# Forget gate's sums brought to the scores by broadcast loads instead of TensorE passes, in a two-layer decoder trunk

## The chip, the cores and the metric

The kernel runs on one core of one Trainium2 chip, as one launch. The metric is the device time of that launch in microseconds (us). The profile shows one execution; the times are those of repeated runs without it. Engines are called as in the profile: PE (TensorE matmul, with PEld its weight loads), DVE (VectorE), ACT (ScalarE), POOL (GpSimd), SP (SyncE, which here only issues DMAs).

## The reference

A decoder trunk of two layers on 256 tokens of width 1024, in fp32. Layer 0 mixes by forgetting attention ("FoX"), layer 1 by MoBA with a relative-position bias. Each is followed by a SwiGLU feed-forward (width 2816) and a gated per-layer embedding; a last RMSNorm ends it. What this case touches is FoX: 16 heads of 64, and in each the logit of query t and key s carries the sum of the log forget gates between them.

```python
log_f = jax.nn.log_sigmoid(f_logit).transpose(0, 2, 1)
...
c = jnp.cumsum(log_f, axis=-1)
...
logits = jnp.einsum('bhqd,bhkd->bhqk', qblk, k).astype(jnp.float32) * scale
logits = logits + cq[..., None] - c[:, :, None, :]
logits = jnp.where(key_pos[None, :] <= t[:, None], logits, -jnp.inf)
probs = jax.nn.softmax(logits, axis=-1).astype(v.dtype)
```

The term `cq` is the same for a whole row and drops out of the softmax. What is left is one row of 256 sums per head, the same for all queries, and the causal mask.

## The kernel before

Every fp32 product is made of three matmuls of fp32r halves: each operand is split into a high and a low part, and high x high, high x low and low x high are added in PSUM (`mm3`, lines L95 to L97). The weights, 113 MB of them in raw form, stream from HBM all along: SP issues a load into `raw` (7 buffers), ACT copies it to `whi` (L170, L192, L140), DVE subtracts to get `wlo` (L176, L193, L143), six buffers each, and PE multiplies. So DVE's `wlo` subtractions stand among everything else that DVE does. One `wlo` per layer is made in two halves, the first by POOL (L172) and the second by DVE later (L173).

The engines take their instructions in the order in which the program leaves them; a scheduler sets that order, from the order of the code and from `tc.issue_after` (and `held`, a list of such marks), which put an instruction behind another one. A DMA stands in the queue of the engine that issues it: SP issues the weight loads, POOL the transfers of attention.

`attention(layer, ...)` treats the 16 heads as eight pairs. Per pair `j`:

- `project(j, 0)` and `project(j, 1)`: PE makes queries and keys of the pair (`pq`); DVE scales them to `qkt` (L578), ACT makes `qkh`, DVE `qkl` (L586).
- `scores(...)`: two pairs at once, behind the projections of pair 2, 4 and 6 (`BEHIND`), so that pairs 0 and 1, 2 and 3, 4 and 5 are done in the midst of the projections; pairs 6 and 7 come last. PE fills four banks `sp` (one per head); DVE's eviction (L624) adds a bias from SBUF, takes the row's minimum, and writes `e`; ACT makes the exponentials (L629) and their sums. The scores are negated throughout, so the minimum is the maximum.
- `scaled`: the reciprocal `rc` (L640) and the product with `e`, on ACT (L651), for pair 6 on DVE (L649).
- `turn`: DVE transposes 32 x 32 blocks (`turn`, L666, two instructions a pair). For pairs 0 to 4 POOL writes them to DRAM (`dt`, L677) and reads them back in four DMAs as `pt` (L681); for pairs 5 to 7 four DMAs go directly to `pt` (L673), by POOL, for pair 7 by SP.
- `values(j)`: PE multiplies `pt` with `v` for pairs j and j + 1 (`po`, L696 and L698), ACT and DVE split the result into `o` (L326, L327).
- `wo`: PE multiplies `o` with the output weights.

The last scores of pairs 6 and 7 are issued with `then=(0, 2)`: PE runs `values(0)` and `values(2)` right behind them, then a piece of `v`, then `wo` for the first pairs. DVE has the evictions of pairs 6 and 7, the splits of `po_0` and `po_2`, the scaling and turning of pairs 6 and 7 and the late half of `wlo` (L173) in that stretch.

In layer 0 the bias of L624 is only the mask `con[:, 0:256]`, whose first half is zero (first 128 columns) and whose second is the triangle. The sums come in by PE: `fox_bias`'s `summed` makes them along the 256 positions (`cum`, L410), ACT and DVE split them into `c` (L412, L414), POOL copies a part (L415), and `add` multiplies `c` by a selector `sel` that is one at the head's row, broadcast to all 128 outputs. This starts each bank `sp`:

```python
def add(i, sp):
    d = slice(i % 2 * DH, i % 2 * DH + DH)
    return mm(sp[:, 0:3 * P], sel[d, i:i + 1].to_broadcast([DH, P]), c[d], start=True, stop=False,
              skip_group_check=True)
```

A bank holds 384 columns: 128 for the first 128 queries with the first 128 keys, 256 for the later 128 queries. In layer 1 the bias is a loaded table (`bias1`), and no such pass is made.

Of the kernel before, what the change touches and what calls it, by code (L numbers as in the profile page):

```python
# [36 lines left out]
H = 16  # L37
# [34 lines left out]
CON = 9 * LINE  # L72
REL = 4 * P + H + 1
# [3 lines left out]
def trunk(ctx: ExitStack, tc: tile.TileContext, xg, wx, xr, pt, w, cst, gf, hot, out):  # L77
# [229 lines left out]
    mask, ident, wf32 = con[:, 0:2 * P], con[:, 2 * P:3 * P], con[:, 3 * P:4 * P].rearrange("p (k h) -> p k h", h=H)  # L307
    sel32, bfs = con[:, 4 * P:4 * P + H], con[:, 4 * P + H:4 * P + H + 1]
    nc.sync.dma_start(con, cst)
    first += [half() for _ in range(2)]  # L310
    sel = tiny.tile([P, H], F32R, bufs=1, name="sel")
    nc.gpsimd.tensor_copy(sel, sel32)
# [58 lines left out]
    def fox_bias(nm):  # L371
# [34 lines left out]
        def summed(f, a):  # L406
            with tc.issue_after(state["low"].ins):
                nc.vector.scalar_tensor_tensor(f, f, 0.0, a, op0=ALU.min, op1=ALU.subtract)
            cum = one.tile([P, S], F32, name="cum")
            nc.vector.tensor_tensor_scan(cum, f, zero, 0.0, ALU.add, ALU.add)  # L410
            c = one.tile([P, 3 * P], F32R, name="c")
            nc.scalar.activation(c[:, P:], cum, AF.Copy)  # L412
            for r in (slice(32, 64), slice(96, 128)):
                nc.vector.tensor_tensor(c[r, P:], cum[r], f32(c[r, P:]), op=ALU.subtract)  # L414
            nc.gpsimd.tensor_copy(c[:, 0:P], c[:, P:2 * P])  # L415

            def add(i, sp):
                d = slice(i % 2 * DH, i % 2 * DH + DH)
                return mm(sp[:, 0:3 * P], sel[d, i:i + 1].to_broadcast([DH, P]), c[d], start=True, stop=False,
                          skip_group_check=True)  # L420

            return (lambda i: (mask[:, P:], mask)), add
# [13 lines left out]
    def moba_bias():  # L436

        pb = bank("pb")
        mm(pb[:, :RVW], rr, hot2, start=True, stop=True)
        rv = work.tile([H, RVW], F32, tag="e", bufs=4, name="rv")  # L440
        nc.vector.scalar_tensor_tensor(rv, pb[:H, :RVW], -1.0, rm, op0=ALU.mult, op1=ALU.add)
        d1 = dram.tile([H, RVW], F32, name="d1")
        nc.sync.dma_start(d1, rv)
        d2 = [dram.tile([P, 4, RVW], F32, name=f"d2_{g}") for g in range(4)]
        bias = []

        def spread(g):
# [12 lines left out]

        return spread, load, (at, None)
# [12 lines left out]
    def attention(layer, nm, mid, early, nf):  # L474
        vb = [bank(f"v{layer}_{b}") for b in range(4)]
        rest, ahead = None, []
# [10 lines left out]
        for c in range(4):  # L487
            wt = [early.pop(0) if early else half() for _ in range(2 if c < 2 else 1)]
            for kk in range(2):
# [8 lines left out]
                if layer == 0 and k == KT - 2:  # L498
                    with tc.issue_after(got.ins), tc.issue_after(state["hi"].ins):
                        nm.spread(-0.125)  # L500
                        nm.column()
                        rest.gather()
                    tail = rest()
                    with tc.issue_after(state["hi"].ins):
                        ahead.append(blocks())
                    bias, add = tail()
# [89 lines left out]
        def scores(*js, then=()):  # L596
# [3 lines left out]
            if add:  # L600
                for i, _, _, sp in heads:
                    add(i, sp)
            for _, d, (t, _, _), sp in heads:
                mm(sp[:, 0:P], t[d, 0, 0:P], t[d, 1, 0:P], start=add is None, stop=True, skip_group_check=True)
# [5 lines left out]
            for i in then:  # L610
                with tc.issue_after(got.ins):
                    got = values(i)
                out = out or marks["o"]
            sl = (slice(0, P), slice(P, 3 * P))
            for n, j in enumerate(js):
# [4 lines left out]
                for s in range(2):  # L620
                    i, _, _, sp = heads[2 * n + s]
                    for q, b in enumerate(bias(i)):
                        with tc.issue_after(out[1].ins) if out and n and s else nullcontext():
                            marks["low"] = nc.vector.tensor_tensor_reduce(e[:, s, sl[q]], sp[:, sl[q]], b, 1.0, 3.0e38,  # L624
                                                                          ALU.add, ALU.min, mn[:, 0, s, q:q + 1])
# [11 lines left out]
        def inverse(j, mn):  # L637

            rc = tiny.tile([P, 2, 2], F32, tag="rc", bufs=4, name=f"rc{layer}_{j}")
            nc.vector.reciprocal(rc, mn[:, 1])  # L640
            return rc

        def scaled(j, e, mn):

            rc = inverse(j, mn)
# [8 lines left out]
        def turn(j, e):  # L654
# [8 lines left out]
            for s in range(2):  # L663
                src = e[:, s].rearrange("p (b y c) -> p b c y", b=3, c=4) if near else \
                      e[:, s].rearrange("p (b c x) -> p b c x", b=3, x=32)
                nc.vector.transpose(t[:, :, :, s].rearrange("p c b x -> p b c x"), src)  # L666
# [22 lines left out]
        def values(j):  # L689
# [9 lines left out]
            src = po.rearrange("p (j s) -> p j s", s=S)  # L699
            marks["o"] = ()  # L700
            for c in (slice(0, 1), slice(1, 2)) if j == 4 else (slice(0, 2),):
                at = slice(j + c.start, j + c.stop)
                marks["o"] += split(oh[:, at], ol[:, at], src[:, c])
            return got

        for j in range(NP):
            project(j, 0)
            if layer and j == 0:
# [5 lines left out]
                bias, add = mid(nm)()  # L714
# [3 lines left out]
            if j + 1 in BEHIND:  # L718
                got = scores(j - 2, j - 1)

# [40 lines left out]
        for x in fresh:  # L761
            scaled(*x)
            turn(*x[:2])
# [404 lines left out]
```

## Time and profile before

| | |
|---|---|
| timed runs, median (lowest to highest), 3 runs | 633.79 us (633.28 to 633.79) |
| the profiled execution's own time | 633.15 us |
| its span | 631.3 us |
| PE's granted clock, mean | 0.997 |
| moved by DMA | 135.34 MB, mean 214 GB/s |

Layer 0's attention lies in about the first 105 us of the span; the scores of layer 1 lie between 349 and 386 us. The columns of the rows below and in the prediction: in the page's groups and the timeline, line of the kernel, engine, operation, output <- input, shape, count, then (groups) busy us and mean ns of one, or (timeline, where start and duration stand first) in brackets the idle time before it and who ended it. An `x4` in the timeline stands for four instructions in a row. In the chain of waits a row has its start, its duration and the work that was the last to be waited for. In the rows of DMA issues the last number is the median time from issue to landing, in us.

```profile
PE   9999999999999999999999999999999999999995
DVE  6888987986666666668895899699666666666696
POOL 1103350000000000000000045100000000000011
DMA  9867968597766666665675598657766666665512
```

The span in forty slices (15.8 us each), busy tenths. POOL works in two places, the two attentions, and the DMA engines are at their fullest there too.

### The profile page before, as it was taken

The numbers are of one execution on the slowest core, as the hardware profiler recorded it, in microseconds if no ns is written. First come the engines' busy times: TensorE is split into PE (matmuls) and PEld (weight loads), VectorE is DVE, ScalarE is ACT, GpSimd is POOL, SyncE is SP. The second block draws the span as 40 slices with busy tenths as digits, with TensorE's granted clock in tenths as the row PEclk, the third lists the DMA queues.
The fourth block names the chain that finished last, engine by engine and source line by source line (L and its number), as shares of the span: only waits on it lengthen the run. The fifth ranks groups of instructions, "written<-read, shape, count | busy, mean of one in ns | idle before, by whom it ended". The sixth has DMA issues, their size and how long they took to land.

```text
span 631.3 us, 13134 instructions
## 1 busy us (share of the span) xinstructions
PE 623.3 (99%) x5259; PEld 603.9 (96%) x5259; DVE 469.1 (74%) x765; ACT 381.8 (60%) x658; POOL 47.5 (8%) x88
## 2 busy tenths in 40 slices
PE   9999999999999999999999999999999999999995
PEld 7899989999999999999989998999999999999985
DVE  6888987986666666668895899699666666666696
ACT  6768867854444445448774799578444444454653
POOL 1103350000000000000000045100000000000011
PEclk9999999999999999999999999999999999999998
DMA  9867968597766666665675598657766666665512
GB/s 337 297 204 228 282 191 288 177 343 272 241 196 198 193 192 211 198 212 177 193 224 183 199 298 252 213 205 266 240 194 185 199 198 202 196 210 181 168 44 91
DMA packets 41773, 135.34 MB, mean 214 GB/s; under 512 B 5152, under 2 KB 10672, under 8 KB 41712
## 3 DMA queue, kind: packets, MB, share of 16 engines
q1 hardware_dynamic: 37504, 124.18, 60.8%
q0 software_dynamic: 3488, 9.44, 5.1%
q10 hardware_dynamic: 720, 0.89, 0.5%
q8 instruction: 41, 0.67, 0.4%
q14 instruction: 20, 0.16, 0.1%
HBM read 126.07 MB, written 8.15 MB: 213 GB/s over the span
## 4 chain that ended last, share of the span: by engine, by line
PE 92%; DVE 4%; issue 1%; DMA 1%; POOL 1%; ACT 0%; SPq 0%; POOLq 0%; DVEq 0%; ACTq 0%
PE gu L96 13%; PE gu L95 13%; PE gu L97 13%; PE fo L97 6%; PE fo L96 6%; PE fo L95 6%; PE pq L95 5%; PE pq L97 5%; PE pq L96 5%; PE wo L95 2%; PE wo L97 2%; PE v L470 2%; PE wo L96 2%; PE v L95 2%; PE v L96 2%; PE v L97 2%
## 5 line engine op out<-in xcount | busy, mean ns | idle before, releaser
L176 DVE TENSOR_TENSOR wlo<-raw,whi 128x1024 fp32r<-128x1024 f32 (+1 forms) x168 | 203.4, 1216 | 61.1 <-ACT whi L170 61.0
L170 ACT ACTIVATE whi<-raw 128x1024 fp32r<-128x1024 f32 x168 | 175.7, 1056 | 87.9 <-issue 41.4
L96 PE MATMUL gu<-g,whi 128*128 128x256 f32 x704 | 194.6, 276 | 0.0
L95 PE MATMUL gu<-g,whi 128*128 128x256 f32 x704 | 194.6, 276 | 0.0
L97 PE MATMUL gu<-g,wlo 128*128 128x256 f32 x704 | 194.5, 276 | 0.0
L97 PEld LDWEIGHTS gu<-g,wlo 128*128 128x128 f32 x704 | 132.3, 188 | 0.0
L95 PEld LDWEIGHTS gu<-g,whi 128*128 128x128 f32 x704 | 132.2, 188 | 0.0
L96 PEld LDWEIGHTS gu<-g,whi 128*128 128x128 f32 x704 | 132.2, 188 | 0.0
L97 PE MATMUL fo<-fp,wlo 128*128 128x256 f32 x352 | 97.3, 276 | 0.0
L96 PE MATMUL fo<-fp,whi 128*128 128x256 f32 x352 | 97.2, 276 | 0.0
L95 PE MATMUL fo<-fp,whi 128*128 128x256 f32 x352 | 97.2, 276 | 0.0
L95 PE MATMUL pq<-g,whi 128*128 128x256 f32 x256 | 71.4, 279 | 0.0
L96 PE MATMUL pq<-g,whi 128*128 128x256 f32 x256 | 70.7, 276 | 0.0
L97 PE MATMUL pq<-g,wlo 128*128 128x256 f32 x256 | 70.7, 276 | 0.0
L193 DVE TENSOR_TENSOR wlo<-raw,whi 128x1080 fp32r<-128x1080 f32 x36 | 46.0, 1281 | 29.6 <-ACT whi L192 29.0
L95 PEld LDWEIGHTS fo<-fp,whi 128*128 128x128 f32 x352 | 66.1, 188 | 0.0
L96 PEld LDWEIGHTS fo<-fp,whi 128*128 128x128 f32 x352 | 66.1, 188 | 0.0
L97 PEld LDWEIGHTS fo<-fp,wlo 128*128 128x128 f32 x352 | 66.1, 188 | 0.0
L192 ACT ACTIVATE whi<-raw 128x1080 fp32r<-128x1080 f32 x36 | 39.4, 1102 | 26.8 <-PE gu L96 26.8
L95 PEld LDWEIGHTS pq<-g,whi 128*128 128x128 f32 x256 | 48.1, 188 | 0.9
L96 PEld LDWEIGHTS pq<-g,whi 128*128 128x128 f32 x256 | 48.1, 188 | 0.1
L97 PEld LDWEIGHTS pq<-g,wlo 128*128 128x128 f32 x256 | 48.1, 188 | 0.0
(199 smaller groups left out, 1048.9 us busy)
## 6 DMA issues: line engine op xcount, KB each, us to landing
raw<-w SPq DMA_DIRECT2D x177, 512.0 KB, 4.2
raw<-w SPq DMA_DIRECT2D x36, 540.0 KB, 4.0
dt<-turn POOLq DMA_DIRECT2D x10, 384.0 KB, 3.5
pt<-dt POOLq DMA_DIRECT2D x40, 96.0 KB, 5.4
d<-d SPq DMA_DIRECT2D x4, 768.0 KB, 6.7
bias<-d SPq DMA_DIRECT2D x4, 512.0 KB, 7.9
pt<-turn POOLq DMA_DIRECT2D x16, 96.0 KB, 3.0
pt<-turn SPq DMA_DIRECT2D x8, 96.0 KB, 2.9
```

The costliest lines, as they stand in the source:

```text
L95: mm(o, ah, bh, start=start, stop=False, skip_group_check=True)
L96: mm(o, ah, bl, start=False, stop=False, skip_group_check=True)
L97: return mm(o, al, bh, start=False, stop=stop, skip_group_check=True)
L170: state["hi"] = state[f"hi{i}"] = nc.scalar.activation(hi[:, c], raw[:, c], AF.Copy)
L176: state["low"] = nc.vector.tensor_tensor(lo[:, c], raw[:, c], f32(hi[:, c]), op=ALU.subtract)
L192: nc.scalar.activation(ht, raw[:, 0:WW], AF.Copy)
L193: state["lo"] = nc.vector.tensor_tensor(lt, raw[:, 0:WW], f32(ht), op=ALU.subtract)
L470: got = mm(bks[2 * t + hf], x[a][:, t * P:(t + 1) * P], w[b][:, hf * HC:(hf + 1) * HC], start=k + a + b == 0, stop=k + b == KT, skip_group ...
```

## The change

The passes `add`, the tensor `c` and the selector `sel` go, and with them the zero half of the mask (the constants shrink from 576 to 448 columns). In their place:

- POOL writes `cum[0:16]` (16 x 256) to a DRAM tensor `rows`.
- `load(j)`, once per pair: one SP DMA reads the two rows of the pair and broadcasts them to all 128 partitions (128 x 512, 256 KB) into a part of `h` (which is not yet used for anything else); the parts alternate with `j % 2`. Two POOL additions then put the mask on, one writing a copy for the first 128 queries (`first`), one in place (`both`).
- The eviction's bias is `first` and `both`; it adds sums and mask together.
- `load(0)` and `load(1)` follow the sums at once; `load(j)` and `load(j + 1)` follow the scores at j = 2, 4 and 6. The additions of these wait for the load, and the load for the evictions that read the same part before.

Beside that, for both layers, the work behind the last scores is put in another order: both evictions of `e_7` stand behind the split of `po_0`, whose ACT part now stands ahead of the exponentials; the split of `po_2` is put off until pair 6 has been turned, and pair 7 is turned behind it.

```diff
-            c = one.tile([P, 3 * P], F32R, name="c")
-            nc.scalar.activation(c[:, P:], cum, AF.Copy)
-            for r in (slice(32, 64), slice(96, 128)):
-                nc.vector.tensor_tensor(c[r, P:], cum[r], f32(c[r, P:]), op=ALU.subtract)
-            nc.gpsimd.tensor_copy(c[:, 0:P], c[:, P:2 * P])
...
-            return (lambda i: (mask[:, P:], mask)), add
+            rows = dram.tile([H, S], F32, name="rows")
+            nc.gpsimd.dma_start(rows, cum[0:H])
+            low = {}
+
+            def load(j):
+
+                part = h[:, j % 2 * 3:j % 2 * 3 + 3].rearrange("p m s -> p (m s)")
+                first = part[:, 0:S].rearrange("p (s k) -> p s k", k=P)
+                both = part[:, S:].rearrange("p (s k) -> p s k", k=S)
+                nc.sync.dma_start(both, bass.AP(tensor=rows.tensor, offset=rows.offset + 2 * j * S,
+                                                ap=[[0, P], [S, 2], [1, S]]))
+                for to, c in ((first, slice(0, P)), (both, slice(P, S))):
+                    nc.gpsimd.tensor_tensor(to[:, :, c], both[:, :, c], mask.unsqueeze(1).to_broadcast([P, 2, P]),
+                                            op=ALU.add)
+                for i in range(2):
+                    low[2 * j + i] = first[:, i], both[:, i]
+
+            return low.get, load
...
-                    bias, add = tail()
+                    bias, load = tail()
+                    for j in range(2):
+                        load(j)
...
-            if add:
-                for i, _, _, sp in heads:
-                    add(i, sp)
             for _, d, (t, _, _), sp in heads:
-                mm(sp[:, 0:P], t[d, 0, 0:P], t[d, 1, 0:P], start=add is None, stop=True, skip_group_check=True)
+                mm(sp[:, 0:P], t[d, 0, 0:P], t[d, 1, 0:P], start=True, stop=True, skip_group_check=True)
...
-                    got = values(i)
-                out = out or marks["o"]
+                    got = values(i, i != then[0])
+                out = marks["o"]
...
-                        with tc.issue_after(out[1].ins) if out and n and s else nullcontext():
+                        with tc.issue_after(out[1].ins) if out and n else nullcontext():
...
-                        with tc.issue_after(out[0].ins) if out and n == 0 and s else nullcontext():
+                        with tc.issue_after(out[0].ins) if out else nullcontext():
...
+            if late:
+                state["out"] = out
+            else:
+                out()
...
             if j + 1 in BEHIND:
                 got = scores(j - 2, j - 1)
+                for i in (j, j + 1) if load else ():
+                    load(i)
...
-        for x in fresh:
-            scaled(*x)
-            turn(*x[:2])
+        six, seven = fresh
+        scaled(*six)
+        rc = inverse(seven[0], seven[2])
+        with tc.issue_after(marks["rc"].ins):
+            turn(*six[:2])
+        with tc.issue_after(marks["turn"].ins):
+            state["out"]()
+        scaled(*seven, rc)
+        with tc.issue_after(marks["o"][1].ins):
+            turn(*seven[:2])
         state["late"]()
```

In the instruction lists below a number behind an underscore only tells tiles of one name apart; the pair is the first number of `dt_2`, `turn_2`, `e_4`, `po_2`. POOL's list in layer 0 between the transfers of pair 1 and those of pair 4, before:

```order
L681 DMA pt_1_668<-dt_1_669 32x4x192 x4
L677 DMA dt_2_873<-turn_2_869 128x768
L677 DMA dt_3_879<-turn_3_875 128x768
L681 DMA pt_2_872<-dt_2_873 32x4x192 x4
L681 DMA pt_3_878<-dt_3_879 32x4x192 x4
L677 DMA dt_4_1071<-turn_4_1067 128x768
```

and now:

```order
L684 DMA pt_1_671<-dt_1_672 32x4x192 x4
L421 TENSOR_TENSOR h<-h,con 128x256
L421 TENSOR_TENSOR h<-h,con 128x2x128
L421 TENSOR_TENSOR h<-h,con 128x256
L421 TENSOR_TENSOR h<-h,con 128x2x128
L680 DMA dt_2_878<-turn_2_874 128x768
L680 DMA dt_3_884<-turn_3_880 128x768
L684 DMA pt_2_877<-dt_2_878 32x4x192 x4
L684 DMA pt_3_883<-dt_3_884 32x4x192 x4
L421 TENSOR_TENSOR h<-h,con 128x256
L421 TENSOR_TENSOR h<-h,con 128x2x128
```

The four additions for pairs 4 and 5 stand ahead of `dt_2`, and those for pairs 6 and 7 ahead of `dt_4` (before pair 0's transfers stand eight more, for pairs 0 to 3).

DVE's list in layer 0 at the evictions of pairs 2 and 3 (`e_2` from the banks `sp_4` and `sp_5`), before:

```order
L586 TENSOR_TENSOR qkl_4_731<-qkt_4_728,qkh_4_730 128x384
L176 TENSOR_TENSOR wlo_841<-raw_839,whi_840 128x1024
L624 ISA e_2_758,mn_2_759<-sp_4_734,con 128x128
L624 ISA mn_2_759 128x1
L624 ISA e_2_758,mn_2_759<-sp_4_734,con 128x256
```

and now:

```order
L592 TENSOR_TENSOR qkl_4_734<-qkt_4_731,qkh_4_733 128x384
L627 ISA e_2_757,mn_2_758<-sp_4_737,h 128x128
L627 ISA mn_2_758 128x1
L627 ISA e_2_757,mn_2_758<-sp_4_737,h 128x256
L627 ISA mn_2_758 128x1
```

The evictions have moved ahead of one `wlo`, which now follows them; the same holds at the evictions of pairs 0 and 1 and of pairs 4 and 5.

DVE's list in layer 0 behind the last scores, from the first `wlo` behind the evictions of pair 7 to the late half L173, before:

```order
L176 TENSOR_TENSOR wlo_1184<-raw_1182,whi_1183 128x1024
L327 TENSOR_TENSOR o_336<-po_2_1151,o_336 128x2x256
L640 RECIPROCAL rc_6_1194<-mn_6_1163 128x4
L640 RECIPROCAL rc_7_1208<-mn_7_1173 128x4
L649 TENSOR_SCALAR e_6_1162<-e_6_1162,rc_6_1194 128x128
L649 TENSOR_SCALAR e_6_1162<-e_6_1162,rc_6_1194 128x256
L649 TENSOR_SCALAR e_6_1162<-e_6_1162,rc_6_1194 128x128
L649 TENSOR_SCALAR e_6_1162<-e_6_1162,rc_6_1194 128x256
L666 STREAM_TRANSPOSE turn_6_1200<-e_6_1162 128x3x4x32 x2
L666 STREAM_TRANSPOSE turn_7_1214<-e_7_1172 128x3x4x32 x2
L173 TENSOR_TENSOR wlo_1190<-raw_1188,whi_1189 128x512
```

and now:

```order
L176 TENSOR_TENSOR wlo_1185<-raw_1183,whi_1184 128x1024
L643 RECIPROCAL rc_6_1195<-mn_6_1164 128x4
L652 TENSOR_SCALAR e_6_1163<-e_6_1163,rc_6_1195 128x128
L652 TENSOR_SCALAR e_6_1163<-e_6_1163,rc_6_1195 128x256
L652 TENSOR_SCALAR e_6_1163<-e_6_1163,rc_6_1195 128x128
L652 TENSOR_SCALAR e_6_1163<-e_6_1163,rc_6_1195 128x256
L643 RECIPROCAL rc_7_1201<-mn_7_1174 128x4
L669 STREAM_TRANSPOSE turn_6_1203<-e_6_1163 128x3x4x32 x2
L325 TENSOR_TENSOR o_337<-po_2_1154,o_337 128x2x256
L669 STREAM_TRANSPOSE turn_7_1217<-e_7_1173 128x3x4x32
L173 TENSOR_TENSOR wlo_1191<-raw_1189,whi_1190 128x512
L669 STREAM_TRANSPOSE turn_7_1217<-e_7_1173 128x3x4x32
```

The split of `po_2` has gone behind pair 6's transposes, and L173 stands ahead of the last of the four transposes instead of behind it. On SP the four transfers of `pt_7` now stand behind one more weight load (540 KB).

More of the change, by code (lines that the diff above doesn't have):

```diff
@@ L71 @@
 GX = 64 + S
-CON = 9 * LINE
-REL = 4 * P + H + 1
+CON = 7 * LINE
+REL = 3 * P + H + 1
 @with_exitstack
@@ L306, in trunk @@
     con = one.tile([P, CON], F32, name="con")
-    mask, ident, wf32 = con[:, 0:2 * P], con[:, 2 * P:3 * P], con[:, 3 * P:4 * P].rearrange("p (k h) -> p k h", h=H)
-    sel32, bfs = con[:, 4 * P:4 * P + H], con[:, 4 * P + H:4 * P + H + 1]
+    mask, ident, wf32 = con[:, 0:P], con[:, P:2 * P], con[:, 2 * P:3 * P].rearrange("p (k h) -> p k h", h=H)
+    sel32, bfs = con[:, 3 * P:3 * P + H], con[:, 3 * P + H:3 * P + H + 1]
     nc.sync.dma_start(con, cst)
     first += [half() for _ in range(2)]
-    sel = tiny.tile([P, H], F32R, bufs=1, name="sel")
-    nc.gpsimd.tensor_copy(sel, sel32)
     rl = con[0:2 * BUCKETS, REL:REL + H]
@@ L410, in summed @@
             nc.vector.tensor_tensor_scan(cum, f, zero, 0.0, ALU.add, ALU.add)
-            c = one.tile([P, 3 * P], F32R, name="c")
-            nc.scalar.activation(c[:, P:], cum, AF.Copy)
-            for r in (slice(32, 64), slice(96, 128)):
[L414 to L420, printed above, removed]
-            return (lambda i: (mask[:, P:], mask)), add
+            rows = dram.tile([H, S], F32, name="rows")
[13 more added lines that the diff above has]
+            return low.get, load
         rest.gather = gather
@@ L459, in at @@
             return bias[0][:, i, P:2 * P], bias[0][:, i]
-        return spread, load, (at, None)
+        return spread, load, at
     def enter(bks, x, w, k):
@@ L475, in attention @@
         vb = [bank(f"v{layer}_{b}") for b in range(4)]
-        rest, ahead = None, []
+        rest, ahead, load = None, [], None
         def row(k, hf, w):
@@ L639, in inverse, with scaled @@
             rc = tiny.tile([P, 2, 2], F32, tag="rc", bufs=4, name=f"rc{layer}_{j}")
-            nc.vector.reciprocal(rc, mn[:, 1])
+            marks["rc"] = nc.vector.reciprocal(rc, mn[:, 1])
             return rc
-        def scaled(j, e, mn):
-            rc = inverse(j, mn)
+        def scaled(j, e, mn, rc=None):
+            rc = inverse(j, mn) if rc is None else rc
             for s in range(2):
@@ L665, in turn @@
                       e[:, s].rearrange("p (b c x) -> p b c x", b=3, x=32)
-                nc.vector.transpose(t[:, :, :, s].rearrange("p c b x -> p b c x"), src)
+                marks["turn"] = nc.vector.transpose(t[:, :, :, s].rearrange("p c b x -> p b c x"), src)
             p = work.tile([P, 4, 3, 2, 32], F32, tag="pt", bufs=4, name=f"pt{layer}_{j}")
@@ L687, in attention, with values @@
         pts = {}
-        def values(j):
+        def values(j, late=False):
             po = bank(f"po{layer}_{j}")
@@ L698, in values, with out @@
                     got = mm(o[d, P:S], v[:, 1, c], t[:, 2], start=False, stop=True, skip_group_check=True)
[L699 to L703, printed above, removed]
+            def out():
+                src = po.rearrange("p (j s) -> p j s", s=S)
+                marks["o"] = ()
+                for c in (slice(0, 1), slice(1, 2)) if j == 4 else (slice(0, 2),):
+                    at = slice(j + c.start, j + c.stop)
+                    marks["o"] += split(oh[:, at], ol[:, at], src[:, c])
+            if late:
+                state["out"] = out
+            else:
+                out()
             return got
@@ L713, in attention @@
                 keep(0)
-                bias, add = mid(nm)()
+                bias = mid(nm)()
             project(j, 1)
@@ L1142 @@
     hot, rvm = _buckets()
-    cst = np.concatenate([np.zeros((P, P), np.float32), tri, np.eye(P, dtype=np.float32),
+    cst = np.concatenate([tri, np.eye(P, dtype=np.float32),
                           fw[:, 3 * D:].reshape(KT, P, H).transpose(1, 0, 2).reshape(P, P),
```

## The prediction

> **What bounds the kernel now.** I read the page first (busy shares, chain), then the chain of waits in one score stage of each layer, then the timelines of PE, POOL and DVE through layer 0's attention, and last the DMA issues there.
>
> ```profile
> PE 623.3 (99%) x5259; PEld 603.9 (96%) x5259; DVE 469.1 (74%) x765; ACT 381.8 (60%) x658; POOL 47.5 (8%) x88
> PE 92%; DVE 4%; issue 1%; DMA 1%; POOL 1%; ACT 0%; SPq 0%; POOLq 0%; DVEq 0%; ACTq 0%
> ```
>
> PE is the bound: 99% busy and 92% of the chain. Taking a PE pass away therefore pays in full, as long as nothing PE needs then comes late. Everything below is that question.
>
> **The sum is made against the profiled execution**: 633.15 us, of which 631.3 is the span. The three timed runs have a median of 633.79 (633.28 to 633.79), so it lies 0.64 under the median. To speak of medians I add half of that, 0.3, to its result. A measurement of this kernel tells about 0.2% from no change, 1.27 us.
>
> **1. The sixteen passes go.** The chain through one score stage of layer 0, and through one of layer 1, which has no such passes, is what the new stage looks like:
>
> ```profile
> 53.33 0.54 PE sp L419 x4
> 53.88 0.45 PE sp L604 x8
> 54.32 0.71 PE sp L607 x12
> ...
> 362.36 0.65 PE sp L604 x8
> 363.01 0.71 PE sp L607 x12
> ```
>
> Layer 0's stage lasts 0.54 + 0.45 + 0.71 = 1.70 us, layer 1's 0.65 + 0.71 = 1.36: the first pass after the projections is slower, whichever it is. So a stage wins 0.34, less than the 0.54 that the passes take in the chain. Four stages: 4 x 0.34 = **-1.4 us**.
>
> The work that made `c` (ACT copy, two DVE subtractions, POOL cast) goes too. PE never waited for it, so I price it at nothing; the same for the smaller constant load and for the eviction's second operand, which is read from SBUF before and after.
>
> **2. Order behind the last scores.** Here is the one wait of PE in this attention, and what DVE does ahead of it:
>
> ```profile
> 88.97 0.28 PE L95 MATMUL wo<-o,whi 128*128 128x256 f32 x1
> ...
> 90.44 0.28 PE L96 MATMUL wo<-o,whi 128*128 128x256 f32 x1
> 91.15 0.38 PE L97 MATMUL wo<-o,wlo 128*128 128x256 f32 x1 [0.43 <-DVE wlo L173]
> 91.37 0.29 PE L95 MATMUL wo<-o,whi 128*128 128x256 f32 x1
> ...
> 87.35 3.17 DVE L666 STREAM_TRANSPOSE turn<-e 128x384 f32<-128x384 f32 x4
> 90.44 0.66 DVE L173 TENSOR_TENSOR wlo<-raw,whi 128x512 fp32r<-128x512 f32 x1
> ```
>
> Two steps take 0.93 us here and 0.23 elsewhere (matmuls start 0.11 apart), so 0.70 is lost. The new order puts one of the four transposes (3.17/4 = 0.79) behind L173. DVE's chain starts from the scores and so moves with PE; L173 then comes 0.79 earlier against PE and the wait goes: **-0.7 us**. Late next would be the split of `po_2` (`o`), which now stands behind the first two transposes, with the third between it and L173: L173 starts at 90.44 - 1.4 - 0.79 = 88.25, so the split ends at 87.46. PE begins the part of `wo` that reads it at 88.97 - 1.4 = 87.57, so this gain is all there is. In layer 1 no wait stands there and none is gained. In both layers `pt_7`'s four SP transfers now stand behind one more weight load (540 KB):
>
> ```profile
> 90.58 2.57 SPq L673 DMA_DIRECT2D pt<-turn  x4
> ...
> pt<-turn SPq DMA_DIRECT2D x8, 96.0 KB, 2.9
> ...
> 97.22 0.60 PE L696 MATMUL po<-pt,v 128*64 128x256 f32 x4
> ```
>
> The last one starts about 92.5 and lands at 95.4; PE reads at 97.2. Its transpose comes 1.4 earlier with the stage and 0.6 later for L173 ahead of it, so 94.6, plus up to 1.9 behind the load (540 KB at the 280 GB/s of the windows row in 5): 94.6 to 96.5, against 97.2 - 2.1 = 95.1 if PE waits nowhere. I price it at nothing in the forecast, since a wait in term 5 gives it room, with 1.4 as upper end.
>
> With nothing late the sum is -2.1 us, 631.05 on the profiled execution.
>
> **3. What is added.** Per pair: a broadcast load of 128x512 (256 KB) on SP and two POOL adds of 256 elements. No row shows such an add; the nearest are these, with a cast that ran alone and one that ran beside a two-input DVE instruction:
>
> ```profile
> 18.62 0.90 POOL L388 TENSOR_TENSOR qs<-quarters,qs 128x256 fp32r<-128x256 f32 x1 [4.65 <-ACT qs L387]
> 12.71 0.29 POOL L379 CAST add<-con 128x128 fp32r<-128x128 f32 x1
> 35.08 1.27 POOL L415 CAST c<-c 128x128 fp32r<-128x128 f32 x1 [14.65 <-DVE c L414]
> 34.98 1.23 DVE L176 TENSOR_TENSOR wlo<-raw,whi 128x1024 fp32r<-128x1024 f32 x1
> ```
>
> The same cast took 0.29 alone and 1.27 while DVE's subtraction ran, so a POOL instruction can sit out a whole DVE one. I take 0.90 for an add (same shape), with 0.6 and 1.3 as ends.
>
> The Trainium skill, "GPSIMD Engine Reference", section 3.1, speaks against this change: an elementwise add belongs on the Vector engine, and GpSimd needs about 2.6 cycles an element, by which 256 elements would be an estimated 0.55 us. That is less than the 0.90 of the trace; by the page the wait worked out in 5 would be 0.7 shorter.
>
> **4. The first pairs.** Their terms come from these rows:
>
> ```profile
> 31.79 0.69 DVE L410 TENSOR_TENSOR_SCAN cum<-f,zero 128x256 f32<-128x256 f32 x1
> 44.22 0.27 DVE L624 CUSTOM_DVE_ANT_0 e<-sp,con 128x128 f32<-128x128 f32 x1
> ...
> d<-rv SPq DMA_DIRECT2D x1, 24.0 KB, 2.3
> raw<-w SPq DMA_DIRECT2D x1, 512.0 KB, 3.6
> ```
>
> The sums are ready at 32.5. Writing 16 KB to DRAM, issue and landing (0.55 + 2.3) gives 35.4; a broadcast load at most as long as a 512 KB one, and the second queued right behind it, gives 39.4; four adds of 0.9 to 1.3 end between 43.0 and 44.6. The first eviction, which now stands ahead of one 1.2 us subtraction, would start at 43.1 and needs only the first pair's two adds (41.2 to 42). Cost: nothing, up to 1 us if the loads land in a crowd.
>
> **5. The later pairs, where POOL's queue decides.** The adds for pairs 4 and 5 now stand on POOL ahead of `dt_2<-turn_2`; behind that are `dt_3` and the eight `pt<-dt` that `values(2)` reads on PE.
>
> ```profile
> 55.81 1.23 DVE L176 TENSOR_TENSOR wlo<-raw,whi 128x1024 fp32r<-128x1024 f32 x1
> 58.83 0.42 DVE L624 CUSTOM_DVE_ANT_0 e<-sp,con 128x256 f32<-128x256 f32 x1
> ...
> 64.59 0.56 POOL L677 DMA_DIRECT2D dt<-turn  x1 [5.35 <-DVE turn L666]
> 65.52 0.56 POOL L677 DMA_DIRECT2D dt<-turn  x1 [0.36 <-DVE turn L666]
> 68.82 4.37 POOL L681 DMA_DIRECT2D pt<-dt  x8 [2.74 <-DMA dt<-turn]
> ...
> 79.89 0.60 PE L696 MATMUL po<-pt,v 128*64 128x256 f32 x4
> ...
> pt<-dt POOLq DMA_DIRECT2D x2, 96.0 KB, 6.5
> raw<-w SPq DMA_DIRECT2D x1, 512.0 KB, 5.9
> raw<-w SPq DMA_DIRECT2D x1, 512.0 KB, 7.7
> ...
> 68.00:74.00 6.00, 6.00 (x51) 5.91 (x51) 4.42 (x22) 5.39 (x20) 4.37 (x8) 1.00 0.93 280
> ```
>
> Before: the last of the eight starts at 68.82 + 7 x 0.55 = 72.6 and lands 6.5 later, at 79.1. PE reads pair 3 at 79.89: a margin of 0.8 us. PE now comes 1.4 earlier, at 78.5. If nothing else changed, the transposes would come two stages' worth (0.7) earlier and `pt_3` land at 78.4: margin nothing.
>
> After: pair 5's load reuses the buffer of pair 3, whose last eviction ended at 59.2. It now ends 0.7 earlier for PE and 1.2 earlier for the subtraction (55.81) that no longer stands ahead: 57.3. The load goes out then, among weight loads that took 5.9 and 7.7 us (issued at 55.4 and 57.1); I take 5.9, since it has half their bytes but queues behind them, with 3.6 and 7.7 as ends: landed at 63.2. Two adds, 1.8: 65.0. Then `dt_2` and, 0.6 later, `dt_3` at 65.6, where 65.52 was before. So `pt_3` lands at 79.2 rather than 78.4. The loads of pairs 6 and 7 (0.5 MB) go out near 69 to 70, into the stretch in which DMA is 93% busy at 280 GB/s: 1.9 us of all engines, half of it felt by the transfers that share them, 0.9. Landed: 80.1. PE waits 80.1 - 78.5 = **+1.6 us**. The ends: no wait; and 65.0 + 2.6 for slow adds = 67.6, `dt_3` 68.2, `pt_3` at 81.8, with all 1.9 us felt 83.7, a wait of 5.2.
>
> While PE waits there, L173 and `po_2` have that much more room, so term 2 stays. Pairs 6 and 7 get their adds after `pt_3`'s issues; a late `e_7` has the same room. Later `dt_4` and `pt_4`, two to three us late, are read only 15 us after. The weight loads behind SP's new waits are used some 10 us or more after their issue: nothing.
>
> **Sum**: -1.4 - 0.7 + 1.6 = -0.5 us, 632.65 profiled, **633.0 us** as a median.
>
> **The rivals.**
>
> *The waits stay hidden (faster).* If pair 5's load lands in 4 us and the adds take 0.6, POOL is free before the transposes are done, the wait at `values(2)` is under 0.8, and `pt_7` is not late by more. Time: between -2.1 and -1.3, 631.4 to 632.2. For it: the load has half a weight load's bytes, and the eight `pt` of the first pairs leave the DMA sooner or later than assumed. Against it: a margin of nothing even without a delay.
>
> *DVE and POOL hold each other up (slower).* These rows are one operation on DVE, in layer 0 beside POOL's subtraction and in layer 1 without it:
>
> ```profile
> 85.36 2.07 DVE L649 TENSOR_SCALAR e<-e,rc 128x128 f32<-128x128 f32 x4
> 85.99 1.29 POOL L172 TENSOR_TENSOR wlo<-raw,whi 128x512 fp32r<-128x512 f32 x1 [2.15 <-DVE e L649]
> ...
> 392.98 1.01 DVE L649 TENSOR_SCALAR e<-e,rc 128x128 f32<-128x128 f32 x4
> 393.90 3.19 DVE L666 STREAM_TRANSPOSE turn<-e 128x384 f32<-128x384 f32 x4
> ...
> 393.85 1.30 POOL L172 TENSOR_TENSOR wlo<-raw,whi 128x512 fp32r<-128x512 f32 x1 [1.07 <-DVE e L649]
> ...
> 44.00:80.00 36.00, 36.00 (x337) 34.14 (x337) 31.36 (x91) 31.07 (x87) 12.42 (x23) 1.00 0.84 258
> ```
>
> DVE lost 1.06 us to 1.29 us of POOL. If each add costs DVE as much of its own length, 0.74, the twelve adds between 44 and 80 us cost it 8.9; by the windows view DVE is busy there for 31.36 of 36 us, idle for 4.6, so it would fall 4.3 behind and PE with it: -2.1 + 4.3 = +2.2, **635.6**. It decides once more than (4.6 + 2.1 + 1.3)/12 = 0.67 us of each add falls on DVE. For it: most of DVE's time there is two-input subtractions. Against it: evictions and transposes are in between (layer 1's POOL subtraction at 393.85 left the four transposes at 3.19, against 3.17 in layer 0), and most adds wait for DVE instead of holding it. The Trainium skill, "SBUF — State Buffer", section "Who interferes with whom", gives the rule: a DVE instruction with two SBUF inputs and a GpSimd instruction that reads SBUF share a read port, and whichever issues first keeps it. The trace agrees (1.27 for 0.29, 2.07 for 1.01).
>
> *POOL's queue at its slow end (slower)* is case 5's upper end, +1.3 to +3.1: 634.8 to 636.6.
>
> *The change doesn't do what it says*: no; the passes are gone from PE's program, and only the price of what replaces them is open.
>
> **How the numbers follow.** A small wait at `values(2)` that eats most of the gain (between -1.3 and +1.3): 0.42; hidden: 0.36; DVE and POOL together 0.12; queue's slow end 0.10. So faster 0.36, same 0.42, slower 0.22. The likeliest case alone spans 632.2 to 634.7. The range takes in the hidden case to its floor, 633.15 - 2.1 + 0.3 = 631.35, and the slower cases up to DVE's price: 631.3 to 635.6; what lies beyond is 1 in 10.
>
> **What would show it.** Score stages of layer 0 of 1.36 us (term 1); no wait on L173 (term 2); first eviction not waiting for POOL (4); `pt_3` landing near 80 and PE waiting at `po` L696 near 78.5 (5); adds near 0.9 us, DVE's subtractions still near 1.2. I am wrong if PE does not wait at L696 although `dt_2` is late, or waits for `wlo` in the projections instead.

## The result, and the profile after

The changed kernel is slower: a median of 639.88 us in six runs (638.02 to 641.90) against 633.51 for the kernel before in its six, a ratio of 1.0109 with a 95% interval of 1.0097 to 1.0120. That is 6.4 us between the medians and 6.9 by the ratio, outside the range of 631.3 to 635.6. It was run once more beside later experiments:

> The changed kernel once more on the chip of these runs, for a comparison on one chip and a second trace: 638 to 642 us, the wait before pair 2 or 3 in layer 0 between 5 and 8 us, and any further loss at another place, layer 1 among them.

1.0079 (1.0051 to 1.0108), with waits of 4.6 and 1.2 us before pairs 2 and 3 in layer 0 and none in layer 1. All ratios are of fast runs; of the seven runs of "`dt` first" below, one took 1620.93 us and is not in its ratio. The profiled execution took 640.03 us, its span 638.2 (before: 633.15 and 631.3).

The page of the changed kernel: busy shares, the granted clock of PE in forty slices, the shares of the chain, and the DMA issues of the new loads.

```profile
PE 623.7 (98%) x5243; PEld 602.7 (94%) x5243; DVE 469.0 (73%) x763; ACT 382.1 (60%) x657; POOL 61.9 (10%) x103
...
PEclk9999979999999999999999999999999999999999
...
PE 84%; DVE 6%; DMA 5%; issue 2%; POOL 1%; ACT 1%; SPq 1%; POOLq 0%; DVEq 0%; ACTq 0%
...
h<-rows SPq DMA_DIRECT2D x8, 256.0 KB, 6.0
```

Sixteen matmuls are gone, but PE's busy time has not fallen and DMA has taken 5% of the chain. The place is one: from the first projection to `values(4)` PE needed 71.4 us before (23.8 to 95.2) and 78.4 now (23.3 to 101.7); what follows lasts as long as before (536.1 and 536.5 us to the end of the span).

PE's timeline at the values behind the last scores:

```profile
75.15 0.71 PE L607 MATMUL sp<-qkt 64*128 64x128 f32 x8
...
76.51 0.65 PE L699 MATMUL po<-pt,v 128*64 128x256 f32 x4
...
83.44 1.12 PE L699 MATMUL po<-pt,v 128*64 128x256 f32 x4 [5.41 <-DMA pt<-dt]
...
85.47 1.12 PE L699 MATMUL po<-pt,v 128*64 128x256 f32 x4 [0.48 <-DMA pt<-dt]
```

The score stage lasts 76.51 - 75.15 = 1.36 us, as forecast. Then PE stands before pair 2 until 83.44 and before pair 3 until 85.47, waiting for the transfers that POOL issues. POOL's timeline shows why they are late:

```profile
63.68 4.91 POOL L421 TENSOR_TENSOR h<-h,con 128x256 f32<-128x256 f32 x4 [4.61 <-DMA h<-rows]
68.54 1.13 POOL L680 DMA_DIRECT2D dt<-turn  x2
75.13 4.37 POOL L684 DMA_DIRECT2D pt<-dt  x8 [5.46 <-DMA dt<-turn]
```

POOL waits 4.61 us for a load, spends 4.91 on the four additions of pairs 4 and 5, and only then issues `dt_2` and `dt_3`, 3.95 us later than before (64.59). These take longer too, and the eight `pt` go out at 75.13 instead of 68.82.

The wait costs more than its length. The windows view (PE busy, then further engines, with PE's granted clock third from the end) and the matmuls show it:

```profile
75.00:80.00 5.00, 3.03 (x37) 2.21 (x36) 4.10 (x7) 3.62 (x7) 4.85 (x9) 1.00 1.00 321
80.00:85.00 5.00, 1.55 (x8) 0.85 (x8) 4.31 (x20) 4.07 (x17) 4.67 (x9) 0.71 0.92 273
85.00:90.00 5.00, 4.53 (x17) 3.33 (x18) 3.81 (x9) 2.63 (x6) 2.93 (x6) 0.61 0.82 235
90.00:95.00 5.00, 5.00 (x42) 4.83 (x42) 4.64 (x6) 3.27 (x4) 3.04 (x5) 1.00 0.66 162
```

With PE idle the clock that it is granted falls to 0.71 and then 0.61 for the first work behind the wait; the four passes at 85.47 take 1.12 us where the same took 0.60 before.

### The profile page after: what moved, and what is told of

The parts are those of the page before. It is cut to its first block, busy times and chain, and to the rows that moved or that the text cites. A ratio compares the mean times of both kernels' runs of the same rounds, so it can differ in the third digit from the quotient of the medians.

```text
span 638.2 us, 13150 instructions
## 1 busy us (share of the span) xinstructions
PE 623.7 (98%) x5243; PEld 602.7 (94%) x5243; DVE 469.0 (73%) x763; ACT 382.1 (60%) x657; POOL 61.9 (10%) x103
## 2 busy tenths in 40 slices
DMA packets 42957, 137.39 MB, mean 215 GB/s; under 512 B 5296, under 2 KB 10960, under 8 KB 42896
## 4 chain that ended last, share of the span: by engine, by line
PE 84%; DVE 6%; DMA 5%; issue 2%; POOL 1%; ACT 1%; SPq 1%; POOLq 0%; DVEq 0%; ACTq 0%
PE gu L96 13%; PE gu L95 13%; PE gu L97 13%; PE fo L97 6%; PE fo L96 6%; PE fo L95 6%; PE pq L95 3%; PE pq L96 3%; PE pq L97 3%; PE wo L95 2%; PE wo L97 2%; PE wo L96 2%; DVE wlo L176 2%; PE v L95 2%; PE v L96 1%
## 5 line engine op out<-in xcount | busy, mean ns | idle before, releaser
L95 PE MATMUL pq<-g,whi 128*128 128x256 f32 x256 | 71.4, 279 | 0.0
```

What stands on the lines that cost most here:

```text
L95: mm(o, ah, bh, start=start, stop=False, skip_group_check=True)
```

## The experiments

Three theories, with what each names as the cause; the expectations call them theory 1, 2 and 3. **Queue** (1): POOL's additions for pairs 4 and 5 wait for their loads and hold `dt_2` and `dt_3` behind them. **Bytes** (2): 2 MB of broadcast loads crowd the other transfers. **Hold-up** (3): POOL's additions and DVE's two-input instructions make each other wait. From here on every run is told as its ratio to the kernel before, measured beside it (there its medians were 632.8 to 633.0 us; 0.0010 is 0.63 us). Each run left one profiled execution, and its place among the run's times is said where it lies at an end.

| run | POOL's additions | bytes of the loads | ratio (95% interval) |
|---|---|---|---|
| change, first set | ahead of `dt_2` | all | 1.0109 (1.0097 to 1.0120) |
| change, second set | ahead of `dt_2` | all | 1.0079 (1.0051 to 1.0108) |
| `dt` first | behind `dt_3` | all | 1.0051 (1.0030 to 1.0072) |
| no additions | none | all | 1.0021 (1.0007 to 1.0036) |
| no loads | ahead of `dt_2` | pairs 0, 1 | 1.0014 (1.0003 to 1.0026) |
| short loads, `dt` first | behind `dt_3` | pairs 0, 1 | 0.9994 (0.9984 to 1.0003) |
| short loads, no additions | none | pairs 0, 1 | 0.9969 (0.9960 to 0.9979) |
| no passes, nothing instead | none | none | 0.9968 (0.9956 to 0.9980) |
| new order alone | (before) | none | 0.9986 (0.9977 to 0.9995) |
| six buffers, early | behind `dt_1` and `dt_3` | all | 1.0004 (0.9995 to 1.0013) |
| six buffers, late additions | behind `dt_3` and `pt_3` | all | 0.9999 (0.9989 to 1.0010) |

### The two gains

The kernel before without its passes:

```diff
-            if add:
-                for i, _, _, sp in heads:
-                    add(i, sp)
...
-                mm(sp[:, 0:P], t[d, 0, 0:P], t[d, 1, 0:P], start=add is None, stop=True, skip_group_check=True)
+                mm(sp[:, 0:P], t[d, 0, 0:P], t[d, 1, 0:P], start=True, stop=True, skip_group_check=True)
```

> The kernel before without its sixteen PE passes and with nothing in their place (the forget gate's sums are left out of the scores). What the passes cost alone. By my first term: each score stage of layer 0 lasts 1.36 us instead of 1.70, together -1.4 us. The wait for the late half of wlo stays about as it is, so the time is 632.0 to 632.4 us against 633.5. If PE then finds pair 3's transposed scores not there (they would land at 78.4 against 78.5), some of it is lost.

0.9968, which is -2.0 us (-2.8 to -1.3). The chain through the same score stage as in the prediction:

```profile
52.34 0.65 PE sp L601 x8
52.99 0.71 PE sp L604 x12
```

1.36 us for 1.70. From the first projection to `values(4)` it is 2.1 us shorter than before. That is more than the -1.4 expected, because the wait for the late half of `wlo` is gone as well: PE waits nowhere up to 110 us.

The kernel before with only the new order behind the last scores:

```diff
-                    got = values(i)
-                out = out or marks["o"]
+                    got = values(i, i != then[0])
+                out = marks["o"]
...
-        for x in fresh:
-            scaled(*x)
-            turn(*x[:2])
+        six, seven = fresh
...
+        with tc.issue_after(marks["turn"].ins):
+            state["out"]()
+        scaled(*seven, rc)
+        with tc.issue_after(marks["o"][1].ins):
+            turn(*seven[:2])
```

> The kernel before with only the new order behind the last scores, passes kept. By my second term: PE's wait of 0.43 us (0.70 lost) for the late half of wlo in layer 0 goes, -0.7 us, 632.8 us. A rival: the split of po_2, put off behind two transposes, comes late for PE instead, and the time is that of before.

0.9986, -0.9 us (-1.5 to -0.3). PE's steps at the place of the wait are 0.11 us all along:

```profile
89.85 0.28 PE L96 MATMUL wo<-o,whi 128*128 128x256 f32 x1
89.96 0.28 PE L97 MATMUL wo<-o,wlo 128*128 128x256 f32 x1
90.07 0.28 PE L95 MATMUL wo<-o,whi 128*128 128x256 f32 x1
```

The rival (a late `po_2`) fell. But the two gains do not add up to more than the first alone brought: without passes the wait went by itself, and the run with both (short loads, no additions) has 0.9969.

### Bytes and additions, one at a time

The changed kernel without its additions (the causal mask of layer 0 is left out):

```diff
-                for to, c in ((first, slice(0, P)), (both, slice(P, S))):
-                    nc.gpsimd.tensor_tensor(to[:, :, c], both[:, :, c], mask.unsqueeze(1).to_broadcast([P, 2, P]),
-                                            op=ALU.add)
...
-                    low[2 * j + i] = first[:, i], both[:, i]
+                    low[2 * j + i] = both[:, i, 0:P], both[:, i]
```

> The changed kernel without its sixteen POOL additions: the loads stay, the evictions read the loaded rows directly, and the causal mask of layer 0 is left out. Theory 1 (POOL's queue: the additions for pairs 4 and 5 wait for their loads and hold up dt_2 and dt_3 behind them): dt_2 is issued near 63.7 us instead of 68.5, pt_3 has landed by 79 to 80.5, PE waits 0.5 to 2 us before the values of pair 3 instead of 7, and the time is 631.5 to 633.5 us. Theory 2 (traffic: 2 MB of loads crowd the transfers, whoever issues them): dt_2 goes out on time, but its transfers still land late, pt_3 after 82, and the time is 635.5 us or more. Theory 3 (DVE and POOL hold each other up at SBUF): as theory 1 in time, since POOL computes nothing there, and DVE's wlo of 1.50 us beside the additions goes back to 1.28.

1.0021: between the two. `dt_2` went out on time, at 63.79, and PE still waited, 0.4 us before pair 2 and 0.8 before pair 3. DMA issues from 63 to 70 us (KB each, median us to landing), first of this run, then of the run without passes:

```profile
dt<-turn POOLq DMA_DIRECT2D x2, 384.0 KB, 5.9
```

```profile
dt<-turn POOLq DMA_DIRECT2D x2, 384.0 KB, 2.8
```

The same two transfers, issued half a microsecond apart in the two runs (63.79 and 63.28), take twice as long when the loads are there. So bytes cost something by themselves, or the weight loads do that wait behind the loads on SP. The next run separates these: the same waits, but 8 partitions instead of 128 for pairs 2 to 7.

```diff
-                nc.sync.dma_start(both, bass.AP(tensor=rows.tensor, offset=rows.offset + 2 * j * S,
-                                                ap=[[0, P], [S, 2], [1, S]]))
+                n = P if j < 2 else 8
+                nc.sync.dma_start(both[0:n], bass.AP(tensor=rows.tensor, offset=rows.offset + 2 * j * S,
+                                                     ap=[[0, n], [S, 2], [1, S]]))
```

> The run without additions, with the loads of pairs 2 to 7 cut from 128 to 8 partitions (16 KB instead of 256 KB each), so that SP's queue has the same waits in the same places and the weight loads behind them go out as late, but 1.4 MB less is moved. The causal mask is left out, and the sums of most rows are those of an earlier pair. Traffic (bytes): 630.5 to 631.5 us, dt lands in about 3 us. The hold-up of the weight loads behind SP's new waits: still 633 to 635, with dt at 5 to 6 us.

0.9969, with `dt` landing in 3.3 us and no wait of PE in either attention. It is the bytes, not SP's queue: 1.0021 - 0.9969 = 0.0052, 3.3 us. ("Bytes" takes in the number of packets, which falls with them, from 42957 to 42189; these runs don't tell the two apart.) The traces, both near the middle of their runs, show 2.4 us between them (633.72 and 631.27). Of these, 1.6 lie between the first projection and `values(4)` of layer 0 (71.0 and 69.4 us) and 0.9 are a wait of PE in layer 1, which comes up again below.

The other half: all additions in their place, the loads of pairs 2 to 7 left out.

```diff
-                nc.sync.dma_start(both, bass.AP(tensor=rows.tensor, offset=rows.offset + 2 * j * S,
+                if j < 2:
+                    nc.sync.dma_start(both, bass.AP(tensor=rows.tensor, offset=rows.offset + 2 * j * S,
```

> The changed kernel with all its POOL additions in their place in the queue, but the loads of pairs 2 to 7 left out (their scores get the sums of pairs 0 and 1 again). Theory 1 (queue order: additions that wait for a load hold up dt): the additions for pairs 4 and 5 wait only for the evictions of pairs 2 and 3 and for pt_1's issues, end by about 64.5, dt_2 goes out at 64 to 64.6 instead of 68.5. Theory 2 (traffic, 3.4 us between the second look at the loads alone and the kernel without passes): with 1.5 MB less, dt and pt land as in the kernel without passes, pt_3 by 76. Both: 631 to 632 us, so this run is for theory 3: if the sixteen additions themselves cost DVE and PE something, the time stays above 632.5 and PE shows waits for wlo.

1.0014, above the 631 to 632 us that queue and bytes gave: the additions cost by themselves. In this run POOL was free before `dt_2`; it waited 1.88 us for DVE's transposes, so the queue held nothing. What is late is DVE. Its `wlo` pair and a PE step that waits for a `wlo`, and then the second of the same two `wlo` instructions in the run with short loads and no additions:

```profile
58.65 2.98 DVE L176 TENSOR_TENSOR wlo<-raw,whi 128x1024 fp32r<-128x1024 f32 x2
...
67.12 0.28 PE L96 MATMUL pq<-g,whi 128*128 128x256 f32 x1
67.42 0.38 PE L97 MATMUL pq<-g,wlo 128*128 128x256 f32 x1
```

```profile
58.77 1.22 DVE L176 TENSOR_TENSOR wlo<-raw,whi 128x1024 fp32r<-128x1024 f32 x1
```

Two such subtractions are 2.36 us where nothing is in the way (2.36 at 45.53 in the changed kernel) and 2.98 beside POOL's additions, which ran from 59.79. DVE was a microsecond behind the run with short loads before that (58.65 for 57.63), and for the same reason: ahead of the first evictions its `qkl` took 1.09 instead of 0.54 us, and behind them a pair of `wlo` 2.97 instead of 2.34, while no eviction waited for POOL. PE's step from 67.12 to 67.42 is 0.30 instead of 0.11, and at 77.06 PE waits 0.30 for a `qkl`. Part of the loss in this run's profile stands in layer 1, where PE waited once for a `pt` transfer (1.0 us; 0.9 in the run without additions). Nothing in layer 1 differs between these runs and the new order alone, which has no such wait; why it came there was not settled. So the prices by ratio may hold some loss that neither bytes nor additions of layer 0 caused.

### The order on POOL

The changed kernel whole, the additions of pairs 4 and 5 put behind `dt_3`:

```diff
+                if j in (4, 5):
+                    state["put"] = state.get("put", []) + [put]
+                else:
+                    put()
...
-                for back in [turn(*x[:2]) for x in far]:
+                backs = [turn(*x[:2]) for x in far]
+                if layer == 0 and j == 5:
+                    with tc.issue_after(marks["dt"].ins):
+                        for put in state.pop("put"):
+                            put()
+                for back in backs:
                     back()
```

> The changed kernel whole, but POOL's additions for pairs 4 and 5 stand behind dt_3 instead of ahead of dt_2. Theory 1 (queue order): dt_2 goes out near 63.8 and dt_3 near 64.7, the additions run while these transfers are under way, pt_3 lands at 79 to 81, PE waits 0.5 to 2.5 us, time 632 to 634.5. Theory 2 (traffic): the order changes little, 635.5 or more. Theory 3 (mutual hold-up): the additions still last about 1.2 us each and DVE's instructions beside them are lengthened; the time lies between, and DVE shows waits in the projections.

1.0051: the order alone was worth 0.0028 (against the second set) to 0.0058 (against the first), 1.8 to 3.7 us, and the kernel is still slower than before. POOL's and PE's timelines:

```profile
64.60 0.56 POOL L691 DMA_DIRECT2D dt<-turn  x1 [5.10 <-DVE turn L680]
65.52 0.56 POOL L691 DMA_DIRECT2D dt<-turn  x1 [0.36 <-DVE turn L680]
66.09 4.42 POOL L422 TENSOR_TENSOR h<-h,con 128x256 f32<-128x256 f32 x4
70.44 4.36 POOL L695 DMA_DIRECT2D pt<-dt  x8
```

```profile
80.48 0.65 PE L710 MATMUL po<-pt,v 128*64 128x256 f32 x4 [1.50 <-DMA pt<-dt]
```

The additions now run while `dt` is under way, and the 5.4 and 0.5 us of waiting are 1.5. This profiled execution, 633.43 us, was the fastest of the six that count, whose median is 636.3; what the usual run waits for stands in no trace. With the bytes cut on top (the diff of the short loads, in this kernel):

> The run with dt first (additions of 4 and 5 behind dt_3), with the loads of pairs 2 to 7 cut to 8 partitions, so that all additions run but 1.4 MB less is moved (most sums are those of an earlier pair). It prices the additions alone at these places. If they cost nothing there: as the short loads without additions, 631 to 631.5 us, ratio 0.997. If DVE and POOL hold each other up there as in the run without loads, 632 to 633. If nearly all of the loss of the run with dt first (ratio 1.005) is traffic, it goes to 0.997 to 0.999 here.

0.9994. Bytes again: 1.0051 - 0.9994 = 0.0057, 3.6 us. And the additions in these places: 0.9994 - 0.9969 = 0.0025, 1.6 us, less than in their place ahead of `dt_2` (1.0014 - 0.9969 = 0.0045, 2.8 us). In its profile, the slowest of its ten runs, PE waited 0.3 us for a `wlo` behind the first evictions, which stood 1.2 us for POOL's first additions, and 0.7 for `pt_7` at `values(6)`.

### Looking for a version that keeps the gain

Six buffers instead of two (`h`, the used `cum`, three free tiles and 3 KB more), so that the loads go out early. First with the additions of pairs 4 and 5 behind `dt_1` and those of 6 and 7 behind `dt_3`:

```diff
+            slots = [(h[:, 0], h[:, 1:3]), (h[:, 3], h[:, 4:6]), (cum, h[:, 6:8])]
+            slots += [(wide[:, k], extra[k]) for k in range(3)]
...
+                first, both = slots[j % 6]
...
-                    for j in range(2):
+                    for j in range(6):
                         load(j)
```

> The changed kernel whole, with six buffers instead of two: the loads of pairs 0 to 5 go out at 36 us, those of 6 and 7 behind the first evictions near 45, where the DMA engines are 53 to 69% busy, and the additions of pairs 4 and 5 stand behind dt_1, those of 6 and 7 behind dt_3. Theories 1 and 2 both say that this takes the loss away: dt_2 near 63.8, pt_3 by 77 to 78.5, no or under 0.5 us of wait, 631 to 632 us, faster than before by 1 to 2 us. If the additions cost DVE its time wherever they stand (theory 3), 633 or more.

1.0004, the same as before. POOL's additions between 54 and 59 us stand beside DVE's subtractions there, and both are longer for it:

```profile
55.54 1.78 POOL L426 TENSOR_TENSOR low<-low,con 128x256 f32<-128x256 f32 x1
57.28 1.06 POOL L426 TENSOR_TENSOR wide<-low,con 128x256 f32<-128x256 f32 x1
58.30 0.74 POOL L426 TENSOR_TENSOR low<-low,con 128x256 f32<-128x256 f32 x1
```

```profile
56.64 1.09 DVE L602 TENSOR_TENSOR qkl<-qkt,qkh 128x384 fp32r<-128x384 f32 x1
```

```profile
61.15 0.38 PE L97 MATMUL pq<-g,wlo 128*128 128x256 f32 x1 [0.18 <-DVE wlo L176]
...
80.99 0.65 PE L714 MATMUL po<-pt,v 128*64 128x256 f32 x4 [0.63 <-DMA pt<-dt]
```

An addition takes 0.74 us alone and up to 1.78; `qkl` takes 1.09 instead of 0.56; PE comes to wait for `wlo`. Its longer wait, 0.63 us, is before pair 3: `dt_2` went out at 66.09, behind DVE's transposes. The longer instructions are what the Trainium skill states in "SBUF — State Buffer", section "Who interferes with whom": a DVE instruction with two SBUF inputs and a GpSimd one that reads SBUF contend for one read port. Beside the evictions, which read one operand from PSUM, the additions kept their 0.74.

Then with the additions of pairs 4 and 5 behind `dt_3` and those of 6 and 7 behind `pt_3`; pairs 2 and 3 take the buffers of 0 and 1:

```diff
+                first, both = slots[j if j < 2 else j - 2]
...
+                if layer == 0 and j == 5:
+                    with tc.issue_after(marks["pt"].ins):
+                        for _ in range(2):
+                            state["put"].pop(0)()
```

> The changed kernel whole with six buffers: the loads of pairs 0, 1 and 4 to 7 go out together at 36 us, those of 2 and 3 behind the first evictions, and the additions of pairs 4 and 5 stand behind dt_3, those of 6 and 7 behind pt_3, where the run with dt first had them and PE showed no wait for wlo. Between 54 and 59 us, where the six early buffers' additions made PE wait for wlo, none stands. Queue, traffic and hold-up together: nothing is left of the loss but some 0.3 us, so 631 to 632 us, 0.15 to 0.3% faster than before. If traffic costs the same wherever the loads stand, 632.5 to 634.

0.9999, the same again; its profiled run was the fastest of twelve (630.73 us, PE waiting nowhere in this attention), the slowest took 634.92. So a good case exists, but it is not what most runs get. In that execution too an addition stood 1.77 us beside DVE's subtractions (at 65.62); so an addition that is held up need not make PE wait.

No arrangement with the loads was measurably faster than the kernel before. The only version with sums and mask complete that was faster than both kernels is the new order alone, 0.9986.

## Why the prediction was wrong

1. *The passes, -1.4 us*: right. 1.36 us a stage for 1.70, in the changed kernel and in the one without passes.
2. *The wait for the late `wlo`, -0.7 us*: right in size where it was tried alone (-0.9). What I did not see is that it goes without the new order too, once the passes are gone. Its side cost, `pt_7` behind one more weight load, which I put at nothing, showed in one trace: 0.7 us at `values(6)`. The sum with nothing late, -2.1 us, is what the runs with neither bytes nor additions have: -2.0.
3. *An addition at 0.90 us, ends 0.6 and 1.3*: the sixteen take 0.97 us on average in the changed kernel (15.0 us in all, as they overlap a little), 0.74 alone and 1.77 at worst; in two other runs one took 2.5. The four of pairs 4 and 5, which the wait hung on, took 4.91 together, 1.23 each. The estimate that the prediction worked out from the Trainium skill, "GPSIMD Engine Reference", section 3.1, 0.55 us, is under what any of them took (0.72 at least).
4. *The first pairs, nothing*: right in the changed kernel, whose first eviction started at 43.21 (43.1 worked out). In another run of the same order they were late and PE waited 0.3 us.
5. *The later pairs, +1.6 us*: the step that failed. The place and the mechanism were named, POOL's queue ahead of `dt_2`; the size was not 1.6, nor under its upper end of 5.2, but 85.47 - 78.5 = 7.0 us to the start of pair 3, and then some 1.5 at the lower clock. By its own terms:
   - The load of pair 5 went out at 58.1 (I had 57.3) and took 6.8 us (I had 5.9).
   - I let only pair 5's two additions stand behind it, 1.8 us. Pair 4's load landed late as well, so all four ran behind that: from 63.68, 4.91 us. `dt_3` left at 69.1, not 65.6: 3.5 us of the miss.
   - I moved `dt` along with its 3.9 us from issue to landing and put 0.9 us for the crowd on the end. It took 6.3 and more; the last `pt` took 6.3 (6.5 before).
   - From `dt_3`'s issue to `pt_3`'s landing that makes 16.2 us for 14.5, another 1.7 of the miss. Together `pt_3` landed near 85.3 instead of 80.1.

```profile
h<-rows SPq DMA_DIRECT2D x1, 256.0 KB, 6.8
dt<-turn POOLq DMA_DIRECT2D x1, 384.0 KB, 6.3
pt<-dt POOLq DMA_DIRECT2D x2, 96.0 KB, 6.3
```

   These are DMA issues of the changed kernel, at 58.1, 68.5 and 78.9 us.
6. *The rivals*: "DVE and POOL hold each other up" was priced at +4.3 us over the gain and given 0.12. It is real and smaller, and it depends on the place: the additions cost 2.8 us ahead of `dt_2` (1.0014 - 0.9969), and 1.6 to 1.9 behind `dt_3` (0.9994 - 0.9969, and 1.0051 - 1.0021). Not all of that need be hold-up: in the trace of the short loads with `dt` first, evictions stood 1.2 us for the additions themselves. A wait for `wlo`, which I had named as a sign of being wrong, is there in both traces of the changed kernel, 0.2 and 0.3 us in the matmuls of `v` near 72.4, beside the much longer waits for `pt`. Of the two pairs of rows that I took as agreeing with the port rule only the cast (1.27 for 0.29) is a clean case; L649, at 2.07 for 1.01, has one tensor and a column of factors as inputs, not two tensors. "Hidden" fell.

   I treated these cases as alternatives, and they add up. Bytes cost 0.0052 without additions and 0.0057 with them; additions behind `dt_3` cost 0.0025 without the bytes and 0.0030 with them. The order on POOL is what is left between the run with `dt` first and the changed kernel, 0.0028 to 0.0058 (1.8 to 3.7 us), so that these terms and the gains of -2.0 us come to the measured +5.0 and +6.9 us by its definition and not as a check. The order's price also takes in that the additions alone cost more ahead of `dt_2` than behind `dt_3`, 2.8 against 1.6 us. By the intervals of the table each of these prices is known to about a microsecond either way, and the intervals behind 2.8 and 1.6 just touch.

By the ratios the bytes were mis-sized by some 2.5 us: 0.9 us in the prediction, 3.3 to 3.6 here, of which the traces place 1.6 in layer 0. The additions on DVE, which the sum put at nothing, cost 1.6 to 2.8. In the trace of the changed kernel most of the miss lies ahead of `dt_3`, in loads that land late and additions that take long. The windows view of the kernel before, from 56 to 80 us (the last two columns are the share of the DMA engines and GB/s), shows how little room there was:

```profile
56.00:80.00 24.00, 24.00 (x224) 22.40 (x224) 20.86 (x61) 20.61 (x58) 10.00 (x19) 1.00 0.95 284
```

Half a megabyte more in it does not take half of its own 1.9 us from each transfer; `dt` took 2.6 us more (3.3 and 5.9 us in the two runs without additions), and `pt` follows `dt`.

## What to carry to other kernels

A transfer into a stretch where the DMA engines are full makes the transfers beside it longer (here, between 56 and 80 us and without additions, `dt` went from 3.3 to 5.9 us and the 512 KB weight loads from 4.9 to 6.5), and the bill is paid at the one whose landing PE awaits with the least margin; price it by what those transfers take with and without it, not by its own bytes. An instruction put ahead in an in-order queue brings its own waits with it: what stands behind gets its release, its length and its slower surroundings, so the queue's later DMAs should be placed first. When several small losses could follow, add them before taking one as the case.

## What the runs showed of the hardware that was not expected

- After 5.4 us of idle PE the granted clock was 0.71 and 0.61 in the next two windows of 5 us, and passes took 1.12 us instead of 0.60. In the second trace of the changed kernel it was 0.57 and 0.50 after 4.6 us; after the wait of 1.5 us with `dt` first it stayed at 1.00. From `values(0)` to `wo` the changed kernel needs 14.2 us (76.5 to 90.7) and the short-load run 5.7 (76.4 to 82.1); of the 8.5 between, 7.0 are the wait until pair 3 starts, and the rest, 1.5, falls in that slow stretch.
- Both bytes and additions widen the spread of the runs: 632.2 to 633.6 us in 25 of the kernel before (632.2 to 634.4 in 23 others) and 630.5 to 631.7 in nine with neither, but 632.2 to 637.0 in ten with the bytes and no additions, 632.2 to 636.3 in ten with the additions ahead of `dt_2` and no later loads, and 630.9 to 633.7 in ten with them behind `dt_3` and short loads. Why was not settled. A single profile of such a kernel can show its good case.
